# RWKV recurrence: values centred per head ahead of the scan, one mask instruction for both matrices of a bank, head norms and rates in two row halves

## The chip, the cores and the metric

The kernel runs on one core of a Trainium2 chip. The metric is the device time of one execution in microseconds (us); lower is better. Three runs of the kernel before took 3750.63, 3755.2 and 3758.21 us, a median of 3755.2 us.

## The reference

The reference is a two-block network over 512 positions of width 1024 with 256 context positions. One block mixes by attention, the other by an RWKV-7 recurrence with 16 heads of 64 values, in both directions; each has a feed-forward part. What the change touches is this part of the second block:

```python
def wkv_scan(r, w, k, v, a, b, s0, reverse):
    def step(s, inp):
        r_t, w_t, k_t, v_t, a_t, b_t = inp
        sa = jnp.einsum('bhvk,bhk->bhv', s, a_t)
        s = s * w_t[:, :, None, :] + sa[..., None] * b_t[:, :, None, :] + v_t[..., None] * k_t[:, :, None, :]
        return s, jnp.einsum('bhvk,bhk->bhv', s, r_t)
...
    a = heads(jax.nn.sigmoid((a0 + (xa @ a1) @ a2).astype(F32)))
    kk = k * k_k.astype(F32).reshape(hn)
    kk = kk / jnp.maximum(jnp.sqrt(jnp.sum(kk * kk, axis=-1, keepdims=True)), 1e-12)
...
def group_norm(y, g, b):
    mean = jnp.mean(y, axis=-1, keepdims=True)
    var = jnp.mean(jnp.square(y - mean), axis=-1, keepdims=True)
    return (y - mean) * lax.rsqrt(var + GN_EPS) * g.astype(F32).reshape(hn) + b.astype(F32).reshape(hn)
```

The output of the scan is normalized per head over its 64 values. The scan is linear in `v`, and its state starts at zero, so that the mean over a head's values of `y` is the scan's answer to the mean of `v`. Values with their mean taken off give an output whose mean is zero.

## The kernel before

The second block's mixer runs in stages, each of which works on eight pairs of heads (128 of the 1024 channels, 768 positions of context and sequence).

- **k projection**, then **features**. `rwkv_features` runs the v and r projections (`psk`, three matmuls for each product of numbers split in a high and a low half) on TensorE, and weaves into them the features of one head pair after another: `psrn` (head norms, spread from the rows of `rnT` by a 32-row matmul), `psa` (rates, from `ta`, a 64-row matmul), `psw` (decays; its two 64-row halves alternate in pieces of 256 columns), `psgt`, `psbon`. The results go to scratch tensors in DRAM (`scr_bk`, `scr_ax`, `scr_ac`, `scr_v`, `scr_z`).
- **Transition**. `rwkv_wkv` takes new SBUF for the recurrence, loads the first pair (`BK`, `DA`, `DC`, `v`) on POOL's and SP's queues, and runs its scores. On POOL's queue behind these stand 16 loads of 512 KB of the weights `ada_w`, which a small product (`psada`) uses.
- **Recurrence**. For pair p, `in_order` deals out the steps of several generators by the table `WKV_ORDER` (`WKV_LAST` for the last pair): matmuls `m`, cross terms `y`, transfer `w` (which makes `FC` and `FT`), the scan `s` of pair p, the readout `z` of pair p-1 (group norm, then the gate), scores `g` and fills `a`, `b`, `v` of later pairs. Between them it spreads the 34 steps of `wkv_inverse` for pair p+1, which runs on VectorE (DVE): it copies 32x32 blocks of the triangular matrices `GA` into `Z`, transposes them into `T` (L2067, L2068), adds 1 to the diagonal (L2070), inverts them by 30 steps of a product `pr` and a sum into `T` (L2077, L2078), transposes back into `TC` and `TS`, and copies out to `TTt`.
- `wkv_scores` makes 20 masked matrices a pair out of 12 PSUM banks `psg`: 12 of `GA` (L1988) and 8 of `E` (L1990), each 128x256.
- `wkv_fill_v` turns the values around by TensorE transposes into `UV` (L2008). `wkv_readout` takes mean (L2235, L2236), difference (L2238, on POOL), square (on ACT), variance (L2242), scales `Y` (L2247), transposes it (`psz`), makes `z` (L2258), multiplies it into `zz` (L2260, on POOL) and adds both directions (L2262). For the last pair these go to DVE.
- **Readout and what follows** use the recurrence's output through `scr_o`.

Of the kernel before, what the change touches and what calls it, by code (L numbers as in the profile page):

```python
# [9 lines left out]
F32 = mybir.dt.float32  # L10
# [8 lines left out]
P = 128  # L19
# [1422 lines left out]
def host_consts3():  # L1442
    f = np.float32
    c = {}
    p = np.arange(P)
    same = (p[:, None] // 64) == (p[None, :] // 64)
    q, k = (p % 64)[:, None], np.arange(64)[None, :]
    m = np.zeros((P, 2, 2, 64), f)
    m[:, 0, 0], m[:, 0, 1] = q <= k, q < k
    m[:, 1, 0], m[:, 1, 1] = q >= k, q > k  # L1450
    c["k_rmask"] = m
    c["k_bones"] = same.astype(f)

    head = np.zeros((P, KT, 32), f)
    headT = np.zeros((3, 32, 3, P), f)
    for a in range(KT):
        for h in range(2):
            head[64 * h:64 * h + 64, a, 2 * (a // 3) + h] = 1
            headT[:, 2 * (a // 3) + h, a // 3, 64 * h:64 * h + 64] = 1
    c["k_head"], c["k_headT"] = head, headT.reshape(96, 3, P)  # L1460
    return c
# [7 lines left out]
WKV_LAST = "y m y m y y z w w z m w m z s w w s z w s z s w w w s s z s z z s z s r s q s q s q s q s"  # L1469
# [23 lines left out]
class Net3(Net2):  # L1493
# [13 lines left out]
    def rwkv_proj(self, x, scr):  # L1507
# [5 lines left out]
        nc.sync.dma_start(self.mask, A["k_rmask"])  # L1513
        M = XW - 2
# [4 lines left out]
        with ExitStack() as s, ExitStack() as s0:  # L1519
            lo_ = self.pool(s, "lora", 1)  # L1520
            tw = self.tw = lo_.tile([P, TT], F32, name="tw")
            ta = self.ta = lo_.tile([64, TT], F32, name="ta")
            rnT = lo_.tile([96, TT], F32, name="rnT")
# [13 lines left out]
            with ExitStack() as s1, ExitStack() as s2:  # L1537
# [18 lines left out]
                for gi, ps_ in enumerate(([0, 1, 2], [3, 4, 5], [6, 7])):  # L1556
# [30 lines left out]
                    for (_, dc, wd), z in zip(segs, ss):  # L1587
                        for j, (p, sq) in enumerate(zip(ps_, sqs)):
                            nc.tensor.matmul(z[32 * j:32 * j + 32, :], lhsT=hd[:, p, :], rhs=sq[:, dc:dc + wd], start=gi == 0, stop=gi == (1 if j == 2 else 2))
                for (_, dc, w), z in zip(segs, ss):  # L1590
                    nc.scalar.sqrt(rnT[:, dc:dc + w], z[0:96, :])
# [70 lines left out]
    def feature_setup(self, s):  # L1662
# [8 lines left out]
        f["headT"] = headT = sp.tile([96, 3, P], F32, name="headT")  # L1671
# [33 lines left out]
    def features(self, p, r, rnT):  # L1705
# [3 lines left out]
        hr = slice(32 * (p % 3), 32 * (p % 3) + 32)  # L1709
# [94 lines left out]
    def rwkv_wkv(self, rest):  # L1804
        nc, A = self.nc, self.A
        with ExitStack() as s:
# [5 lines left out]
            self.E = [cp.tile([P, 5, 2, 8, 64], F32, name=f"E{d}") for d in range(2)]  # L1812
# [219 lines left out]
    def wkv_fill_m(self, u):  # L2032
        nc, GA, UV = self.nc, u["GA"], u["UV"]
        for (s0, n) in ((8, 4), (0, 8)):
            for h in range(2):
                ps = self.psum("psmv")
                for i in range(n):
                    sl = s0 + i
                    for d in range(2):
                        q, kh = slice(64 * d, 64 * d + 64), slice(64 - 64 * d, 128 - 64 * d)  # L2040
                        nc.tensor.matmul(ps[q, i * 64:(i + 1) * 64], lhsT=GA[d][kh, h, sl, :], rhs=UV[kh, h, sl, d, :], start=True, stop=True)
# [16 lines left out]
    def wkv_inverse(self, u):  # L2058
        nc, tl, Z, GA, TTt = self.nc, self.wt, self.Z, u["GA"], self.TTt
# [25 lines left out]
        for d in range(2):  # L2085
            for bl in range(2):
# [3 lines left out]
                put(TTt[q, :, :, 64 * d + 32 * bl:64 * d + 32 * bl + 32], src[q, :, 0:24].rearrange("p t (h s) -> p h s t", h=2))  # L2090
# [131 lines left out]
    def wkv_readout(self, u, parts=((0, 8),)):  # L2222
        nc, tl, psum = self.nc, self.rt, self.psum
        Y, pc = u["Y"], u["pc"]
        side = nc.vector if u["p"] == KT - 1 else nc.gpsimd
        mn, vr = (tl([P, 16], n, 2) for n in ("mn", "vr"))
# [3 lines left out]
        for j0, j1 in parts:  # L2230
            e = slice(2 * j0, 2 * j1)
            y3 = Y[:, j0:j1].rearrange("p j d t -> p (j d) t")
            m, v, q = mn[:, e], vr[:, e], sq[:, e]
# [15 lines left out]
            for d in range(2):  # L2249
# [10 lines left out]
                side.tensor_tensor(zz[:, d, cs], zz[:, d, cs], z, MUL)  # L2260
# [113 lines left out]
```

## Time and profile before

| | before |
|---|---|
| runs (us) | 3750.63, 3755.2, 3758.21; median 3755.2 |
| profiled execution (us) | 3759.0, span 3757.2 |
| PE busy | 3554.0 us (95%) |
| DVE busy | 2065.8 us (55%) |
| ACT busy | 1531.4 us (41%) |
| POOL busy | 726.0 us (19%) |
| the chain that ended last | PE 53%, DVE 9%, ACT 2%, issue 2%, DMA 1% of the span |

The table is read by stage: features last from 1205 to 1365 us of the span, the transition to 1420, the recurrence from there to 1860. Busy shares over the whole span say little on a stage of them.

### The profile page before, as it was taken

The numbers are of one execution on the slowest core, as the hardware profiler recorded it, in microseconds if no ns is written. First come the engines' busy times: TensorE is split into PE (matmuls) and PEld (weight loads), VectorE is DVE, ScalarE is ACT, GpSimd is POOL, SyncE is SP. The second block draws the span as 40 slices with busy tenths as digits, with TensorE's granted clock in tenths as the row PEclk, the third lists the DMA queues.
The fourth block names the chain that finished last, engine by engine and source line by source line (L and its number), as shares of the span: only waits on it lengthen the run. The fifth ranks groups of instructions, "written<-read, shape, count | busy, mean of one in ns | idle before, by whom it ended". The sixth has DMA issues, their size and how long they took to land.

```text
span 3757.2 us, 63564 instructions
## 1 busy us (share of the span) xinstructions
PE 3554.0 (95%) x26108; PEld 2920.4 (78%) x26108; DVE 2065.8 (55%) x3937; ACT 1531.4 (41%) x2956; POOL 726.0 (19%) x588
## 2 busy tenths in 40 slices
PE   7999999999989988889799999998999899989998
PEld 5767877888865657777588889988888799978886
DVE  5556433333457778899454345567444744573346
ACT  5556332222234655556442234354222345442233
POOL 2100033433222010001224440003111200031112
PEclk9999999999989998888899999999999999989999
DMA  5132233222222782322433332122333321223332
GB/s 182 61 103 95 68 99 104 64 65 62 73 88 71 277 298 91 92 80 87 157 118 95 96 95 91 57 63 87 103 97 90 96 64 60 78 79 100 97 95 68
DMA packets 308211, 370.80 MB, mean 99 GB/s; under 512 B 31712, under 2 KB 228304, under 8 KB 305872
## 3 DMA queue, kind: packets, MB, share of 16 engines
q1 hardware_dynamic: 298752, 340.28, 28.7%
q0 software_dynamic: 8912, 26.39, 2.2%
q8 instruction: 205, 3.36, 0.4%
q14 instruction: 86, 0.70, 0.1%
q10 hardware_dynamic: 256, 0.07, 0.0%
HBM read 324.71 MB, written 41.98 MB: 98 GB/s over the span
## 4 chain that ended last, share of the span: by engine, by line
PE 53%; DVE 9%; ACT 2%; issue 2%; DMA 1%; POOL 0%; SPq 0%; DVEq 0%; ACTq 0%; POOLq 0%
PE psu L142 5%; PE psu L141 5%; PE psu L140 5%; PE psy L142 5%; PE psy L140 4%; PE psy L141 4%; PE psj L140 4%; PE psj L142 4%; PE psj L141 4%; DVE T L2078 1%; DVE Tlo L296 1%; DVE pr L2077 1%; PE S L972 1%; PE psk L140 1%; PE psk L141 1%
## 5 line engine op out<-in xcount | busy, mean ns | idle before, releaser
L135 DVE TENSOR_TENSOR wlo<-wraw,whi 128x1024 fp32r<-128x1024 f32 (+1 forms) x402 | 505.3, 1259 | 543.1 <-ACT whi L134 542.4
L134 ACT CAST whi<-wraw 128x1024 fp32r<-128x1024 f32 (+1 forms) x402 | 417.1, 1039 | 920.2 <-PE psy L142 528.2
L140 PE MATMUL psu<-Thi,whi 128*128 128x512 f32 (+1 forms) x1408 | 499.9, 355 | 8.7 <-ACT r L332 6.0
L142 PE MATMUL psu<-Thi,wlo 128*128 128x512 f32 (+1 forms) x1408 | 501.1, 356 | 0.3 <-DVE wlo L135 0.3
L141 PE MATMUL psu<-Tlo,whi 128*128 128x512 f32 (+1 forms) x1408 | 499.6, 355 | 0.0
L140 PE MATMUL psj<-whi,Thi 128*128 128x256 f32 (+1 forms) x1568 | 482.9, 310 | 10.4 <-ACT whi L134 7.6
L142 PE MATMUL psj<-whi,Tlo 128*128 128x256 f32 (+1 forms) x1568 | 473.8, 303 | 2.5 <-DVE Tlo L296 2.5
L141 PE MATMUL psj<-wlo,Thi 128*128 128x256 f32 (+1 forms) x1568 | 474.3, 303 | 1.2 <-DVE wlo L135 1.0
L140 PE MATMUL psy<-whi,uh 128*128 128x512 f32 x1152 | 452.7, 393 | 3.3 <-ACT whi L134 2.0
L142 PE MATMUL psy<-whi,ul 128*128 128x512 f32 x1152 | 455.0, 395 | 0.0
L141 PE MATMUL psy<-wlo,uh 128*128 128x512 f32 x1152 | 452.3, 393 | 0.0
L333 POOL TENSOR_TENSOR q<-r 128x512 f32<-128x512 f32 (+1 forms) x176 | 235.3, 1337 | 880.0 <-ACT r L332 880.0
L140 PEld LDWEIGHTS psj<-whi,Thi 128*128 128x128 f32 x1568 | 300.2, 192 | 27.4 <-ACT whi L134 9.5
L142 PEld LDWEIGHTS psj<-whi,Tlo 128*128 128x128 f32 x1568 | 299.6, 191 | 15.0 <-DVE Tlo L296 4.2
L141 PEld LDWEIGHTS psj<-wlo,Thi 128*128 128x128 f32 x1568 | 300.3, 192 | 13.0 <-DVE wlo L135 2.5
L140 PEld LDWEIGHTS psu<-Thi,whi 128*128 128x128 f32 x1408 | 268.3, 191 | 52.1 <-ACT r L332 8.1
L141 PEld LDWEIGHTS psu<-Tlo,whi 128*128 128x128 f32 x1408 | 268.4, 191 | 40.7
L142 PEld LDWEIGHTS psu<-Thi,wlo 128*128 128x128 f32 x1408 | 268.3, 191 | 38.5 <-DVE wlo L135 0.7
L335 DVE TENSOR_TENSOR ul<-q,uh 128x512 fp32r<-128x512 f32 (+1 forms) x176 | 105.0, 597 | 316.4 <-ACT uh L334 316.1
L142 PEld LDWEIGHTS psy<-whi,ul 128*128 128x128 f32 x1152 | 216.8, 188 | 53.2 <-DVE ul L335 6.5
L140 PEld LDWEIGHTS psy<-whi,uh 128*128 128x128 f32 x1152 | 216.7, 188 | 52.3 <-ACT whi L134 2.4
L141 PEld LDWEIGHTS psy<-wlo,uh 128*128 128x128 f32 x1152 | 216.9, 188 | 47.2
(545 smaller groups left out, 6100.8 us busy)
## 6 DMA issues: line engine op xcount, KB each, us to landing
wraw<-in_mlp_w_dram SPq DMA_DIRECT2D x128, 512.0 KB, 3.9
wraw<-in_ffn_w_dram SPq DMA_DIRECT2D x128, 512.0 KB, 3.8
wraw<-in_ada_w_dram SPq DMA_DIRECT2D x64, 512.0 KB, 4.8
wraw<-in_ev_w_in_dram SPq DMA_DIRECT2D x28, 512.0 KB, 3.6
scr_bk<-BK SPq DMA_DIRECT2D x16, 768.0 KB, 3.3
wraw<-in_od_w_in_dram SPq DMA_DIRECT2D x24, 512.0 KB, 3.6
BK<-scr_bk SPq DMA_DIRECT2D x14, 768.0 KB, 4.7
wraw<-in_rwkv_w_rkv_dram SPq DMA_DIRECT2D x16, 512.0 KB, 4.6
```

The lines of the kernel that those rows point to most:

```text
L134: nc.scalar.copy(hi, raw)
L135: nc.vector.tensor_tensor(lo, raw, hi.bitcast(F32), SUB)
L140: mm(ps, lhsT=ah, rhs=bh, start=start, stop=False)
L141: mm(ps, lhsT=ah, rhs=bl, start=False, stop=False)
L142: mm(ps, lhsT=al, rhs=bh, start=False, stop=stop)
L296: nc.vector.tensor_tensor(lo[k][:, s], t[:, :w], hi[k][:, s].bitcast(F32), SUB)
L333: nc.gpsimd.tensor_tensor(q[:, :w], r[:, :w], r[:, :w], MUL)
L335: nc.vector.tensor_tensor(ul[:, o:o + w], q[:, :w], uh[:, o:o + w].bitcast(F32), SUB)
L972: nc.tensor.matmul(S[e][:, c], lhsT=q[r], rhs=k[r, c], start=True, stop=True)
L2077: nc.vector.tensor_tensor(pv, T[:, j + 1:, j:j + 1].to_broadcast([P, n, j]), T[:, j:j + 1, 0:j].to_broadcast([P, n, j]), MUL)
L2078: nc.vector.tensor_tensor(T[:, j + 1:, 0:j], T[:, j + 1:, 0:j], pv, ADD)
```

## The change

1. Features: `psa` and `psrn` are made together. `rnT` moves into rows 64 to 127 of a tile whose rows 0 to 63 hold `ta`, the table `headT` goes to 64 rows, and the two 64-row matmuls alternate in pieces of 256 columns. The sums of squares that fill `rnT` (`ss`) take columns 64 and 96 in place of 0, 32 and 64.
2. Values: `wkv_fill_v` multiplies by `cent` (the unit matrix less 1/64 within each head) in place of a transpose. The readout loses mean, its scaling, and the difference.
3. Masks: `GA` of the 8 sequence chunks moves into two more slots of `E`, so that one instruction of 512 elements masks both matrices of a bank. `GAc` holds the 4 context chunks. Each copy into `Z` and out to `TTt` becomes two, for 8 and 4 chunks.
4. Inverse: the first and the last of the 30 steps become one instruction each, and the diagonal is set to 1 by a memset after the first.
5. The product into `zz` goes from POOL to DVE for all pairs. `WKV_LAST` has one `q` less.
6. SBUF: each `E` grows from 5 to 7 slots (4 KB each per partition), `GA` gives way to the smaller `GAc`. By that the tiles that are allocated behind `E` start later.

```diff
-            self.E = [cp.tile([P, 5, 2, 8, 64], F32, name=f"E{d}") for d in range(2)]
+            self.E = [cp.tile([P, 7, 2, 8, 64], F32, name=f"E{d}") for d in range(2)]
...
         for (o, w) in segs:
-            ps = psum("psrn")
-            nc.tensor.matmul(ps[:, :w], lhsT=f["headT"][hr, p // 3, :], rhs=rnT[hr, o:o + w], start=True, stop=True)
-            nc.vector.scalar_tensor_tensor(na[:, o:o + w], in0=k[:, o:o + w], scalar=f["nkk"][:, pc], in1=ps[:, :w], op0=MUL, op1=MUL)
-        yield
-        for (o, w) in segs:
-            ps = psum("psa")
-            nc.tensor.matmul(ps[:, :w], lhsT=a2, rhs=self.ta[:, o:o + w], start=True, stop=True)
-            nc.scalar.activation(ic[:, o:o + w], ps[:, :w], AF.Tanh, bias=f["ha0"][:, pc], scale=0.5)
-        nc.scalar.activation(ic, ic, AF.Copy, bias=0.5, scale=0.5)
-        yield
+            pa, pn = psum("psa"), psum("psrn")
+            for c in range(0, w, 256):
+                for ps, l, rhs in ((pa, a2, self.ta), (pn, f["headT"][:, p, :], rnT)):
+                    nc.tensor.matmul(ps[:, c:c + 256], lhsT=l, rhs=rhs[:, o + c:o + c + 256], start=True, stop=True)
+            nc.scalar.activation(ic[:, o:o + w], pa[:, :w], AF.Tanh, bias=f["ha0"][:, pc], scale=0.5)
+            nc.vector.scalar_tensor_tensor(na[:, o:o + w], in0=k[:, o:o + w], scalar=f["nkk"][:, pc], in1=pn[:, :w], op0=MUL, op1=MUL)
...
-                    nc.vector.tensor_tensor(GA[d][:, h, sg4, :], pv[:, :, n - 1, :], mask[:, d, 1, :].unsqueeze(1).to_broadcast([P, 4, 64]), MUL)
-                    if n == 2:
-                        nc.vector.tensor_tensor(self.E[d][:, u["R"][d], h, sg4, :], pv[:, :, 0, :],
-                                                mask[:, d, 0, :].unsqueeze(1).to_broadcast([P, 4, 64]), MUL)
+                    if n == 1:
+                        nc.vector.tensor_tensor(GAc[d][:, h], pv[:, :, 0, :], mask[:, d, 1, :].unsqueeze(1).to_broadcast([P, 4, 64]), MUL)
+                    else:
+                        a, b = u["R"][d], u["A"]
+                        nc.vector.tensor_tensor(self.E[d][:, a:b + 1:b - a, h, sg4, :], pv.rearrange("p s e t -> p e s t"),
+                                                mask[:, d].unsqueeze(2).to_broadcast([P, 2, 4, 64]), MUL)
...
-                nc.tensor.transpose(ps[:, i * P:(i + 1) * P], v[:, c * 64:c * 64 + 128], self.ident)
+                nc.tensor.matmul(ps[:, i * P:(i + 1) * P], lhsT=v[:, c * 64:c * 64 + 128], rhs=self.cent, start=True, stop=True)
...
-                put(Z[q, :, 0:24], GA[d][q, :, :, 32 * bl:32 * bl + 32].rearrange("p h s t -> p t (h s)"))
+                put(Z[q, :, 0:16], self.E[d][q, u["A"], :, :, cs].rearrange("p h s t -> p t (h s)"))
+                put(Z[q, :, 16:24], u["GAc"][d][q, :, :, cs].rearrange("p h s t -> p t (h s)"))
...
-        dg = T.rearrange("p a b -> p (a b)")[:, 0:1024:33]
-        nc.vector.tensor_scalar(dg, dg, 1.0, None, ADD)
...
+            if j in (1, 30):
+                out = T[:, 2:, 0] if j == 1 else T[:, 31, 0:30]
+                nc.vector.scalar_tensor_tensor(out, in0=T[:, 2:, 1] if j == 1 else T[:, 30, 0:30], scalar=T[:, 1, 0:1] if j == 1 else T[:, 31, 30:31],
+                                               in1=out, op0=MUL, op1=ADD)
...
-            nc.vector.tensor_reduce(m, y3, AX.X, ADD)
-            nc.vector.tensor_scalar(m, m, 1.0 / 64, None, MUL)
-            yield
-            side.tensor_tensor(y3, y3, all64(m), SUB)
-            yield
...
-                side.tensor_tensor(zz[:, d, cs], zz[:, d, cs], z, MUL)
+                nc.vector.tensor_tensor(zz[:, d, cs], zz[:, d, cs], z, MUL)
```

Three places show how the instructions move. The first is TensorE in the features of one head pair, first before (`psk` are projection matmuls, the numbers behind names are of buffers):

```order
L1723 MATMUL psrn<-rnT,headT 128x512
L1723 MATMUL psrn<-rnT,headT 128x256
L140 MATMUL psk<-vh,whi 128x512
L141 MATMUL psk<-vl,whi 128x512
L142 MATMUL psk<-vh,wlo 128x512
L1728 MATMUL psa<-ta,a_11578 128x512
L1728 MATMUL psa<-ta,a_11578 128x256
```

The same two products of another head pair with the change:

```order
L1732 MATMUL psa<-tarn,a_10842 128x256
L1732 MATMUL psrn<-tarn,headT 128x256
L1732 MATMUL psa<-tarn,a_10842 128x256
L1732 MATMUL psrn<-tarn,headT 128x256
...
L1732 MATMUL psa<-tarn,a_10842 128x256
L1732 MATMUL psrn<-tarn,headT 128x256
```

Two matmuls of each, on 32 and on 64 rows, have become three of each on 64 rows, which alternate.

The second is VectorE in the recurrence, from the transposes that end one inverse to those that begin the next, before (the part around the second head's masks is left out):

```order
L2083 STREAM_TRANSPOSE TS<-T 128x1024
L1988 TENSOR_TENSOR GA_15602<-psg,rmask 128x256
L1990 TENSOR_TENSOR E_12152<-psg,rmask 128x256
...
L2064 COPY Z<-GA_15602 32x32x24 x2
L2067 STREAM_TRANSPOSE T<-Z 64x1024
...
L2235 TENSOR_REDUCE mn<-Y 128x16
L2068 STREAM_TRANSPOSE T<-Z 64x32x32
L2236 TENSOR_SCALAR mn<-mn 128x16
L2107 COPY y1s<-psy_15917 32x384
L2070 TENSOR_SCALAR T<-T 128x32
```

The same place with the change:

```order
L2106 STREAM_TRANSPOSE TS<-T 128x1024
L2003 TENSOR_TENSOR E_12169<-psg,rmask 128x2x256 x2
...
L2079 COPY Z<-E_12169 32x32x16 x2
L2083 STREAM_TRANSPOSE T<-Z 64x1024
L2000 TENSOR_TENSOR GAc_15586<-psg,rmask 128x256 x2
L2003 TENSOR_TENSOR E_12170<-psg,rmask 128x2x256 x4
L2084 STREAM_TRANSPOSE T<-Z 64x32x32
L2091 SCALAR_TENSOR_TENSOR T<-T 128x30
L2132 COPY y1s<-psy_15895 32x384
L2095 MEMSET T 128x32
```

The mean and the sum on the diagonal are gone, and the `Z` copies of the context chunks (not in these rows) stand between steps of the inverse before.

The third is VectorE where `z` of a pair meets the inverse, with the change; before, `L2258 z` stood here without the product behind it:

```order
L2178 TENSOR_TENSOR FT<-psft,IR 128x512 x2
L2101 TENSOR_TENSOR T<-T,pr 128x14x17
L2277 SCALAR_TENSOR_TENSOR z<-psz,ncol,bv 128x512
L2100 TENSOR_TENSOR pr<-T 128x234
L2279 TENSOR_TENSOR zz<-zz,z 128x512
L2101 TENSOR_TENSOR T<-T,pr 128x13x18
L2281 TENSOR_TENSOR zz<-zz 128x512
```

The product `zz<-zz,z`, an instruction of POOL before, now stands among the steps on VectorE.

## Rows read from the trace of the kernel before

**Rows 1.** Windows by stage: us, busy of PE, PEld, DVE, ACT, POOL, clock, DMA share, GB/s.

```profile
1250.00:1300.00 50.00, 50.00 (x232) 34.86 (x231) 39.01 (x51) 34.77 (x54) 0.00 (x0) 1.00 0.79 264
...
1350.00:1400.00 50.00, 39.60 (x342) 26.64 (x342) 37.14 (x80) 25.48 (x40) 12.43 (x20) 0.86 0.99 365
...
1519.84:1576.83 56.99, 50.24 (x962) 43.78 (x958) 49.60 (x109) 31.68 (x72) 4.52 (x3) 0.82 0.29 88
...
1632.33:1687.00 54.67, 46.95 (x966) 40.99 (x966) 49.59 (x106) 31.49 (x73) 4.51 (x3) 0.91 0.29 92
```

**Rows 2.** Chain that ended last, features: start, us on the chain, what.

```profile
1260.38 1.48 PE psrn L1723 x4
...
1262.76 1.48 PE psa L1728 x4
...
1268.09 1.06 PE psw L1738 x8
...
1270.04 0.63 PE psw L1738 x4
```

**Rows 3.** Timeline of POOL and PE, transition: start, us, operation, [idle before, releaser].

```profile
1348.67 0.53 POOL L1939 DMA_DIRECT2D DA<-scr_ax  x1
...
1364.03 2.09 POOL L221 DMA_DIRECT2D E<-in_ada_w_dram  x4 [14.30 <-DMA scr_z<-gt]
...
1365.93 0.71 PE L1979 MATMUL psg<-DA,BK 64*128 64x128 f32 x4 [1.34 <-ACT vf L1639]
...
1373.16 2.40 PE L1979 MATMUL psg<-DA,BK 64*128 64x128 f32 x16 [4.28 <-DVE GA L1988]
```

**Rows 4.** DMA issues from 1340 to 1370: queue, count, KB, us to landing.

```profile
DA<-scr_ax POOLq DMA_DIRECT2D x1, 1024.0 KB, 14.8
```

**Rows 5.** Timeline of DVE in one period of the recurrence, 1632 to 1687.

```profile
1633.81 0.41 DVE L1990 TENSOR_TENSOR E<-psg,rmask 128x256 f32<-128x256 f32 x1
1634.14 0.41 DVE L1988 TENSOR_TENSOR GA<-psg,rmask 128x256 f32<-128x256 f32 x1
...
1648.04 1.22 DVE L2235 TENSOR_REDUCE mn<-Y 128x16 f32<-128x1024 f32 x1 [1.85 <-ACT Y L2218]
1649.59 1.93 DVE L2068 STREAM_TRANSPOSE T<-Z 64x1024 f32<-64x1024 f32 x1 [0.33 <-ACT Z L2064]
...
1652.34 1.48 DVE L2070 TENSOR_SCALAR T<-T 128x32 f32<-128x32 f32 x1
...
1670.13 1.28 DVE L2153 TENSOR_TENSOR FT<-psft,IR 128x512 f32<-128x512 f32 x2
...
1672.41 1.36 DVE L2078 TENSOR_TENSOR T<-T,pr 128x240 f32<-128x240 f32 x1
1673.81 0.41 DVE L2077 TENSOR_TENSOR pr<-T 128x238 f32<-128x238 f32 x1
...
1682.11 0.68 DVE L2262 TENSOR_TENSOR zz<-zz 128x512 f32<-128x512 f32 x1
```

**Rows 6.** Timeline of POOL and ACT in the same period.

```profile
1651.87 1.90 POOL L2238 TENSOR_TENSOR Y<-Y,mn 128x1024 f32<-128x1024 f32 x1 [25.02 <-ACT y1s L2106]
1672.20 1.31 POOL L2260 TENSOR_TENSOR zz<-zz,z 128x512 f32<-128x512 f32 x1 [18.43 <-DVE z L2258]
...
1648.04 1.52 ACT L2064 COPY Z<-GA 32x768 f32<-32x768 f32 x1
```

**Rows 7.** Timeline of PE in the recurrence, two periods.

```profile
1518.97 0.66 PE L2008 MATMUL psv<-ident,v 128*128 128x128 f32 x4
...
1526.35 1.11 PE L2008 MATMUL psv<-ident,v 128*128 128x128 f32 x4
...
1670.71 2.05 PE L2132 MATMUL pswu<-RH,TTt 128*128 128x128 f32 x16
```

**Rows 8.** Chain that ended last, last pair and tail.

```profile
1826.14 1.88 POOL Y L2238
...
1851.76 1.28 POOL zz L2260
```

More of the change, by code (lines that the diff above doesn't have):

```diff
@@ L1452, in host_consts3 @@
     c["k_bones"] = same.astype(f)
+    c["k_cent"] = (np.eye(P) - same / 64.0).astype(f)
     head = np.zeros((P, KT, 32), f)
-    headT = np.zeros((3, 32, 3, P), f)
+    headT = np.zeros((64, KT, P), f)
     for a in range(KT):
         for h in range(2):
-            head[64 * h:64 * h + 64, a, 2 * (a // 3) + h] = 1
-            headT[:, 2 * (a // 3) + h, a // 3, 64 * h:64 * h + 64] = 1
-    c["k_head"], c["k_headT"] = head, headT.reshape(96, 3, P)
+            head[64 * h:64 * h + 64, a, 2 * (a // 2) + h] = 1
+            headT[32 * (a % 2) + 2 * (a // 2) + h, a, 64 * h:64 * h + 64] = 1
+    c["k_head"], c["k_headT"] = head, headT
     return c
@@ L1513, in rwkv_proj @@
         nc.sync.dma_start(self.mask, A["k_rmask"])
+        self.cent = self.keep.tile([P, P], F32, name="cent")
+        nc.sync.dma_start(self.cent, A["k_cent"])
         M = XW - 2
@@ L1521, in rwkv_proj @@
             tw = self.tw = lo_.tile([P, TT], F32, name="tw")
-            ta = self.ta = lo_.tile([64, TT], F32, name="ta")
-            rnT = lo_.tile([96, TT], F32, name="rnT")
+            both = lo_.tile([P, TT], F32, name="tarn")
+            ta, rnT = both[:64], both[64:]
+            self.ta = ta
             sg = self.sg = lo_.tile([P, 2, SX], F32, name="sg")
@@ L1587, in rwkv_proj @@
                     for (_, dc, wd), z in zip(segs, ss):
-                        for j, (p, sq) in enumerate(zip(ps_, sqs)):
-                            nc.tensor.matmul(z[32 * j:32 * j + 32, :], lhsT=hd[:, p, :], rhs=sq[:, dc:dc + wd], start=gi == 0, stop=gi == (1 if j == 2 else 2))
+                        for p, sq in zip(ps_, sqs):
+                            j = 64 + 32 * (p % 2)
+                            nc.tensor.matmul(z[j:j + 32, :], lhsT=hd[:, p, :], rhs=sq[:, dc:dc + wd], start=p < 2, stop=p >= KT - 2)
                 for (_, dc, w), z in zip(segs, ss):
-                    nc.scalar.sqrt(rnT[:, dc:dc + w], z[0:96, :])
+                    nc.scalar.sqrt(rnT[:, dc:dc + w], z[64:, :])
                 nc.vector.tensor_scalar(rnT, rnT, 1e-12, None, MAX)
@@ L1967, in wkv_scores @@
         BK, DA, DC, mask = u["BK"], u["DA"], u["DC"], self.mask
-        u["GA"] = GA = [self.gp.tile([P, 2, NSLOT, 64], F32, name=f"GA{d}", tag=f"GA{d}") for d in range(2)]
+        u["GAc"] = GAc = [self.gp.tile([P, 2, 4, 64], F32, name=f"GAc{d}", tag=f"GAc{d}") for d in range(2)]
         for d in range(2):
@@ L2040, in wkv_fill_m @@
                         q, kh = slice(64 * d, 64 * d + 64), slice(64 - 64 * d, 128 - 64 * d)
-                        nc.tensor.matmul(ps[q, i * 64:(i + 1) * 64], lhsT=GA[d][kh, h, sl, :], rhs=UV[kh, h, sl, d, :], start=True, stop=True)
+                        nc.tensor.matmul(ps[q, i * 64:(i + 1) * 64], lhsT=self.aref(u, d, kh, h, sl), rhs=UV[kh, h, sl, d, :], start=True, stop=True)
                 nc.scalar.copy(u["RH"][:, h, s0:s0 + n, 64:128], ps[:, :n * 64].rearrange("p (s t) -> p s t", t=64))
@@ L2058, in wkv_inverse @@
     def wkv_inverse(self, u):
-        nc, tl, Z, GA, TTt = self.nc, self.wt, self.Z, u["GA"], self.TTt
+        nc, tl, Z, TTt = self.nc, self.wt, self.Z, self.TTt
         for d in range(2):
@@ L2074, in wkv_inverse @@
             n = 31 - j
-            pr = tl([P, 256], "pr")
+            if j in (1, 30):
+                out = T[:, 2:, 0] if j == 1 else T[:, 31, 0:30]
+                nc.vector.scalar_tensor_tensor(out, in0=T[:, 2:, 1] if j == 1 else T[:, 30, 0:30], scalar=T[:, 1, 0:1] if j == 1 else T[:, 31, 30:31],
+                                               in1=out, op0=MUL, op1=ADD)
+                if j == 1:
+                    nc.vector.memset(T.rearrange("p a b -> p (a b)")[:, 0:1024:33], 1.0)
+                yield
+                continue
+            pr = tl([P, 240], "pr")
             pv = pr[:, :n * j].rearrange("p (a b) -> p a b", b=j)
@@ L2100, in wkv_cross @@
             for sl in range(NSLOT):
-                i = h * NSLOT + sl
+                i = h * 8 + sl if sl < 8 else 16 + h * 4 + sl - 8
                 c = slice(32 * sl, 32 * sl + 32)
-                nc.tensor.matmul(y1[q1, c], lhsT=GA[0][q0, h, sl, 32:64], rhs=TS[q0, :, i], start=True, stop=True)
-                nc.tensor.matmul(y1[q2, c], lhsT=GA[1][q3, h, sl, 0:32], rhs=TC[q3, :, i], start=True, stop=True)
+                nc.tensor.matmul(y1[q1, c], lhsT=self.aref(u, 0, q0, h, sl)[:, 32:64], rhs=TS[q0, :, i], start=True, stop=True)
+                nc.tensor.matmul(y1[q2, c], lhsT=self.aref(u, 1, q3, h, sl)[:, 0:32], rhs=TC[q3, :, i], start=True, stop=True)
             y1s = tl([P, SX], "y1s", 2)[:, :NSLOT * 32]
@@ L2224, in wkv_readout @@
         Y, pc = u["Y"], u["pc"]
-        side = nc.vector if u["p"] == KT - 1 else nc.gpsimd
-        mn, vr = (tl([P, 16], n, 2) for n in ("mn", "vr"))
+        vr = tl([P, 16], "vr", 2)
         sq = tl([P, 16, 64], "ysq", tag="ro")
```

23 lines of the change are left out of this document (15 added, 8 removed).

## The prediction

> **What bounds the kernel now.** I read the windows by stage first, because the share of the whole span averages over stages with different limits. In the features, 1250 to 1300, TensorE (PE) is busy 50.00 of 50 us at the full clock, VectorE (DVE) 39.01, ACT 34.77 and the DMA engines 0.79 of the time: the stage ends when PE has gone through its list [rows 1]. The chain of that stage is PE throughout, and it holds for each head pair 1.48 us of psrn, 1.48 of psa, and 1.06 and 0.63 of psw [rows 2]. In the transition, 1350 to 1400, PE has 39.60 busy and DVE 37.14, but DMA is at 0.99 and moves 365 GB/s: that stage is as long as its bytes [rows 1]. In the recurrence, a period of 54.67 us holds 49.59 us of DVE and 46.95 of PE, ACT 31.49; another holds 49.60 of DVE and 50.24 of PE in 56.99 us, at a clock of 0.82 in place of 0.91 [rows 1]. So DVE, with its inverse, leads there by little, and PE stands close behind it. Six periods have this form, from 1465 to about 1800.
>
> **The change part by part.** The sum is made against the profiled execution's own 3759.0 us, which is 3.8 above the median of the runs, 3755.2.
>
> *Features.* psw moves twice the columns of psa (two 64-row halves that alternate) and takes 1.06 + 0.63 = 1.69 us, little more than psa alone [rows 2]. The new pair of psa and psrn has just that form and column count, so 1.48 + 1.48 becomes 1.69: 1.27 us less for each head pair. PE has no idle time there, so this counts in full. There are 8 pairs; I count 7, since the first stands where the weave with the projection only begins: 8.9 us. The bound below is none at all (the halves do not overlap and psw is quick for another reason), above it 8 pairs, 10.2. DVE at 39 of 50 would be at 39 of 47, ACT lower; neither takes over. The matmuls of `ss` are the same number, at other columns, and come out even.
>
> *Transition.* Before, the first load of DA went out at 1348.67, well before the projections were over, and was 14.8 us on the way [rows 3, 4]. The larger E pushes DA, DC and v into SBUF that still holds the high half of v's input (`vh`), read by the last projection matmuls. So DA now waits for the end of PE's list; before, PE went idle 1.34 us ahead of the first psg at 1365.93, that is at 1364.6 [rows 3]. With the shift of 8.9 the issue falls to about 1355.7. Behind it on POOL's queue stand DC and then the loads of ada_w, the first of which went out at 1364.03 after a wait for the last of the features' stores [rows 3]. DA's 1024 KB thus move out of a stretch with DMA time to spare (0.79 in the window before) into one that is full; at 365 GB/s they take 2.9 us. I take 8.9 - 2.9 = 6.0 gained over features and transition. The lower end: DA lands 14.8 after 1355.7, at 1370.5, which is 4.6 later than psg began before. PE waited 4.28 us for DVE's masks shortly after [rows 3], so that such a delay is just covered, and the gain there is 0. The upper end is 8.9. What DVE saves in the first pair's inverse does not count, since DMA ends that stage; for the rest of the first pair I take 1 (0 to 2).
>
> *Recurrence, one period.* On DVE:
> - T beside POOL: while POOL's product zz ran from 1672.20 for 1.31, a T step of 240 elements took 1.36; the step of 238 next to it took 0.41 [rows 5, 6]. POOL has two of these a period, and the second lands on a T step too: 2 x 0.95 = -1.9.
> - The sum on the diagonal took 1.48, beside POOL's difference of 1.90 which began 0.47 ahead of it [rows 5, 6]. A memset of its 32 elements takes its place; I give it 0.3, under the 0.41 of a step of 238: -1.2.
> - The mean, 1.22 (L2235), stands in a wait: DVE was idle 1.85 ahead of it and 0.33 behind it, until ACT had both Z copies of 768 elements, 1.52 each [rows 5, 6]. With the context part copied earlier, 512 elements each are left, 1.0 each by size: the wait ends 1.0 earlier. So the mean itself gives nothing, and this -1.0. Its scaling, 16 elements, at half of that 0.41: -0.2.
> - Masks: two of 256 elements take 0.74 (0.33 to the next start, then 0.41), one of 512 from PSUM takes 0.64 by FT's two in 1.28 [rows 5]. Eight pairs of them by 0.1, less the stride that the two operands now have: -0.5.
> - First and last step of the inverse, an instruction less each, of 30 elements, at the same 0.2: -0.4.
> - The product zz comes to DVE, two of 512 elements by 0.68 as the sum of zz shows [rows 5], less the overlap: +1.2. Half copies of Z and TTt, four more instructions: +0.3.
>
> Together -3.7. On PE: four psv transposes take 0.66, and eight full matmuls on the same 128x128 f32 shape (pswu, 16 instructions, two for each) 2.05 [rows 7]. That is 0.15 against 0.26, +0.1 each, 12 a period: +1.2. At the lower clock four transposes took 1.11 [rows 7]; if the matmul grows alike, +2.4. Part of it lies in PE's 7.7 idle us of a period, part on the chain, as PE hands the chain to DVE and back: I take 0.7. That leaves -3.0 a period. Bounds: -3.7 + 2.4 = -1.3, all of it on the path; and -4.5, where PE hides it and the earlier ysq also ends a wait. Six periods: -18 (-8 to -27).
>
> Here a rule speaks against the change. The Trainium skill, Perfetto Trace Analysis, section Optimizing Tensor Performance (Transposes), wants a logical transpose done as a transpose and not as a standard matmul; TensorE: Matmul & The Clock Gate, section Terms, calls transpose mode 4 times as fast for FP32. By it a psv matmul would cost 0.59 and the period 5.3 us more of PE; the rows above show 1.7 times, not 4.
>
> *Last pair and tail.* POOL's difference stood on the chain with 1.88 and its product with 1.28 [rows 8]. The first goes; the second becomes 0.68 on DVE: -2.5. The readout has two steps less to wait its turn for: -0.5. I take -3 (-1 to -5).
>
> Sum: -6.0 - 1 - 18 - 3 = -28, that is 3731.0 on the profiled time and 3727 against the median.
>
> **The rivals.**
> - *The late DA eats the features' gain* (DMA 0.99 speaks for it, PE's 4.28 us of cover against it): -22, 3733.
> - *PE takes over in the recurrence.* For it: PE's 50.24 beside DVE's 49.60 in one period, and TC and TS now follow each other, 3.2 us in which DVE frees no score bank. Then -1.3 a period: -6 - 1 - 8 - 3 = -18, 3737. With the rival above, 3743.
> - *psv costs four transposes.* By the price of four of them, 0.66, for each matmul, PE gets 12 x 0.5 = 6 us more a period and passes 53 to 56: the recurrence gains nothing, -6 - 3 = -9, 3746. pswu's rate speaks against it.
> - *Slower: the clock.* A period at clock 0.82 lasted 56.99, one at 0.91 54.67 [rows 1]. If PE waits longer behind TC and TS and is granted the lower clock in all six, the period grows by 2.3 instead of falling: +14, less the tail's 3 and the features' 6 or 0: +5 to +11, 3760 to 3766. It decides once the added wait a period is more than the 3.0 saved. [...]
> - *All of it counts*: -8.9 - 2 - 27 - 5 = -43, 3712.
> - *The halves do not overlap*: no gain in features, and DA still late: -21, 3734.
>
> **How the numbers follow.** Forecast 0.42; late DA 0.14; PE takes over 0.14, both 0.06; psv by four 0.04; no overlap 0.05; all counts 0.11; slower 0.04. 0.2% of this kernel, 7.5 us, is about what a measurement can tell from no change. Same comes from the edges of the cases at 3743 and 3746 and a part of the clock's: 0.07; slower 0.04; faster 0.89. The range takes in the bounds of all terms, 3712 less 2 and 3747.
>
> **What would show it.** The pair psa and psrn at about 1.7 us and 1.3 less between head pairs; DA issued only when the projections end, and the first psg waiting for DMA; no POOL work in the recurrence, no T step over 0.45; the wait for ACT's Z shorter by a microsecond; two TC 52 apart rather than 55; four psv at 1.0. The forecast is wrong if PE is then the longer of the two in a period, if the end of the transition doesn't come earlier by some 6, or if the clock of a period falls.

## The result and the profile after

The changed kernel took 3730.61 us (median of 4 runs, 3728.78 to 3737.26) against 3754.34 before (a fourth run of it took 3753.47): a ratio of 0.994, with a 95% interval of 0.9924 to 0.9956. That is 24 us less, where 28 were forecast. The profiled execution is the slowest of the four, 3737.26, so stages are compared below within a profile, from landmark to landmark, and totals by the medians.

Windows of the changed kernel by stage, with the columns of [rows 1]; the last two are periods of the recurrence, from one TC to the next (TC and TS are the transposes that end an inverse):

```profile
1250.00:1300.00 50.00, 50.00 (x249) 36.26 (x247) 42.20 (x57) 36.02 (x54) 0.00 (x0) 1.00 0.85 290
...
1350.00:1400.00 50.00, 34.20 (x331) 25.01 (x330) 37.50 (x77) 21.08 (x36) 13.61 (x22) 0.80 0.87 317
...
1567.74:1619.71 51.97, 46.78 (x982) 40.87 (x982) 45.63 (x103) 32.50 (x76) 0.00 (x0) 0.97 0.30 96
1619.71:1674.04 54.33, 50.81 (x982) 44.65 (x982) 45.80 (x103) 33.00 (x76) 0.00 (x0) 0.87 0.30 93
```

The features are still TensorE's alone. The window from 1350 to 1400 has lost its full DMA (0.87 for 0.99), which is the first sign that something there waits that did not. In the recurrence DVE fell from 49.6 to 45.7, POOL is empty, and the two periods shown differ: 52.0 us at a granted clock of 0.97, and 54.3 at 0.87, where PE is busy 4 us more on the same instructions.

The features' timeline on PE, one head pair, and the psbon that ends two successive pairs:

```profile
1341.25 0.48 PE L1732 MATMUL psa<-tarn,a 64*128 64x256 f32 x1
1341.26 0.48 PE L1732 MATMUL psrn<-tarn,headT 64*128 64x256 f32 x1
1341.57 0.38 PE L1732 MATMUL psa<-tarn,a 64*128 64x256 f32 x1
...
1242.22 1.02 PE L1802 MATMUL psbon<-rk,bones 128*128 128x512 f32 x2
...
1262.84 1.02 PE L1802 MATMUL psbon<-rk,bones 128*128 128x512 f32 x2
```

psa and psrn start 0.01 apart: the halves run together. From pair to pair 20.62 us pass, where 21.90 had passed (psbon at 1243.76 and 1265.66).

The transition, where [rows 3] stood, on POOL and PE:

```profile
1340.70 1.09 POOL L1945 DMA_DIRECT2D BK<-scr_bk  x2 [138.08 <-PE psk L142]
1356.09 0.53 POOL L1946 DMA_DIRECT2D DA<-scr_ax  x1 [14.30 <-DVE sig L1763]
...
1397.42 1.06 POOL L221 DMA_DIRECT2D E<-in_ada_w_dram  x2 [13.14 <-PE psada L223]
...
1362.46 1.19 PE L1990 MATMUL psg<-DA,BK 64*128 64x128 f32 x4 [5.81 <-DMA DA<-scr_ax]
...
1391.12 1.13 PE L1993 MATMUL psg<-DC,BK 64*64 64x64 f32 x32 [8.40 <-DMA DC<-scr_ac]
```

DA goes out 15 us behind BK instead of right behind it; the row names a scan on DVE (`sig`) that ended just then, but the last projection matmuls end within 0.3 us of it, right ahead of psbon at 1355.63. The two keep this distance in every profile, so that time alone does not tell them apart; the place does: in the kernel's SBUF layout DA now starts on the first byte of `vh`, which those matmuls read, and `sig` lies elsewhere. PE then waits twice: 5.81 us for DA, and 8.40 for DC of the second pair. Behind the second wait stand the psada steps, and behind these POOL's next loads of ada_w. Windows of 10 us show what DMA does meanwhile:

```profile
1350.00:1360.00 10.00, 6.65 (x36) 4.20 (x34) 7.22 (x9) 7.37 (x13) 3.24 (x7) 0.97 0.73 278
...
1390.00:1400.00 10.00, 8.88 (x91) 5.50 (x92) 6.75 (x17) 1.17 (x2) 1.06 (x2) 0.65 0.61 218
```

In a stage that was as long as its bytes before (DMA at 0.99 [rows 1]), 0.27 and 0.39 of 10 us are lost, 6.6 us together.

On DVE and PE in a period, the rows that answer to [rows 5] and [rows 7]:

```profile
1622.68 1.25 DVE L2003 TENSOR_TENSOR E<-psg,rmask 128x512 f32<-128x512 f32 x2
...
1637.02 1.95 DVE L2084 STREAM_TRANSPOSE T<-Z 64x1024 f32<-64x1024 f32 x1 [2.22 <-ACT Z L2079]
1639.00 0.28 DVE L2091 SCALAR_TENSOR_TENSOR T<-T 128x30 f32<-128x30 f32 x1
...
1639.96 0.09 DVE L2095 MEMSET T<- 128x32 f32 x1
```

```profile
1619.48 1.16 PE L2022 MATMUL psv<-cent,v 128*128 128x128 f32 x8
1620.57 0.45 PE L2215 MATMUL pstep<-S,FT 64*64 64x64 f32 x8
...
1623.38 0.66 PE L2041 MATMUL psat<-ident,DA 128*128 128x128 f32 x4 [1.72 <-DVE E L2003]
```

Four psv take 1.09 to the next instruction, for about 0.6. Who waits for whom has shifted. These are DVE's waits for scores over the six periods before, and its two largest waits after (engine, instruction, releaser: us in total, times, longest):

```profile
DVE GA L1988 <- PE psg L1979: 3.4, 3, 2.2
DVE GA L1988 <- PE psg L1982: 0.9, 2, 0.6
```

```profile
DVE E L2003 <- PE psg L1990: 17.1, 12, 2.5
DVE T L2084 <- ACT Z L2079: 13.3, 6, 2.2
```

Before, DVE waited 4.3 us in all for scores. Now it waits 17.1: DVE spends part of what it saved on waiting for PE.

### The profile page after: what moved, and what is told of

Same layout as the page of the kernel before. It is cut to its first block, busy times and chain, and to the rows that moved or that the text cites. A ratio compares the mean times of both kernels' runs of the same rounds, so it can differ in the third digit from the quotient of the medians.

```text
span 3735.5 us, 63689 instructions
## 1 busy us (share of the span) xinstructions
PE 3543.6 (95%) x26236; PEld 2921.2 (78%) x26236; DVE 2035.9 (55%) x3883; ACT 1537.1 (41%) x2988; POOL 694.5 (19%) x567
## 4 chain that ended last, share of the span: by engine, by line
PE 81%; DVE 10%; DMA 4%; ACT 3%; issue 2%; POOL 0%; SPq 0%; ACTq 0%; DVEq 0%; POOLq 0%
PE psy L142 7%; PE psy L140 7%; PE psu L142 7%; PE psy L141 7%; PE psu L140 7%; PE psu L141 7%; PE psj L140 5%; PE psj L142 5%; PE psj L141 5%; PE po L579 2%; PE psk L140 1%; PE S L535 1%; DVE Tlo L296 1%; PE pst L554 1%; PE psk L142 1%
## 5 line engine op out<-in xcount | busy, mean ns | idle before, releaser
L142 PEld LDWEIGHTS psj<-whi,Tlo 128*128 128x128 f32 x1568 | 299.7, 191 | 14.8 <-DVE Tlo L296 4.2
```

The costliest lines, as they stand in the source:

```text
L142: mm(ps, lhsT=al, rhs=bh, start=False, stop=stop)
```

## The experiments

All ran against the kernel before, whose medians beside them were 3754.56, 3754.64 and 3752.53; each has its ratio to it. An interval is some 3 to 6 us to either side, so small differences are read from the profiles' stages. The table gives spans of each profile between landmarks on PE and DVE, in us: from the first psk to the last psbon (k projection and features), from there to psadat (the small product's last step: transition), from there to the last TC (recurrence), and from there to the first psu of the feed-forward part (last pair and tail).

| kernel | median | ratio, interval | to psbon | to psadat | to last TC | to psu |
|---|---|---|---|---|---|---|
| before | 3754.34 | 1 | 310.9 | 57.4 | 375.9 | 122.4 |
| changed | 3730.61 | 0.994, 0.9924 to 0.9956 | 304.5 | 64.6 | 361.5 | 118.7 |
| f_only | 3748.42 | 0.9982, 0.9973 to 0.9992 | 304.4 | 58.7 | 376.2 | 122.0 |
| r_only | 3739.84 | 0.9963, 0.995 to 0.9976 | 311.8 | 63.2 | 361.2 | 119.5 |
| b_da | 3730.01 | 0.9932, 0.9918 to 0.9947 | 304.5 | 59.5 | 358.7 | 122.8 |
| b_da_ord | 3727.18 | 0.9927, 0.9916 to 0.9939 | 304.9 | 54.2 | 359.9 | 119.8 |
| x_mean | 3735.92 | 0.9956, 0.9944 to 0.9968 | 304.5 | 63.6 | 359.8 | 120.0 |
| x_ident | 3717.90 | 0.9903, 0.9888 to 0.9918 | 304.8 | 63.5 | 346.1 | 117.5 |
| x_double | 3734.55 | 0.9953, 0.9941 to 0.9966 | 304.4 | 63.2 | 359.5 | 117.9 |
| x_zzpool | 3744.54 | 0.9971, 0.9962 to 0.998 | 304.5 | 63.9 | 368.7 | 121.7 |
| x_ts | 3734.80 | 0.9951, 0.9938 to 0.9963 | 304.9 | 66.8 | 359.3 | 115.8 |
| x_mask | 3733.09 | 0.9951, 0.9937 to 0.9965 | 304.9 | 65.5 | 359.0 | 117.2 |
| best3 | 3729.98 | 0.9943, 0.9931 to 0.9956 | 305.0 | 54.3 | 359.6 | 122.4 |
| best3d | 3720.78 | 0.9919, 0.9905 to 0.9932 | 304.4 | 54.6 | 354.8 | 124.2 |

Kernels with the same instructions in a stage show how far one profile can be trusted. The transition of the changed kernel and of the seven others with its placing lasts 63.2 to 66.8. The recurrence of changed, r_only, b_da and b_da_ord, which is the same, lasts 358.7 to 361.5, and their last stretch 118.7 to 122.8; the two together vary less, 479.8 to 481.5, against 498.4 before and 498.2 in f_only.

**Where the features' gain went.** f_only is the kernel before with the features' part alone. r_only is the changed kernel with psrn and psa apart again:

```diff
-            pa, pn = psum("psa"), psum("psrn")
-            for c in range(0, w, 256):
...
+            pn = psum("psrn")
+            nc.tensor.matmul(pn[:, :w], lhsT=f["headT"][:, p, :], rhs=rnT[:, o:o + w], start=True, stop=True)
...
+        for (o, w) in segs:
+            pa = psum("psa")
+            nc.tensor.matmul(pa[:, :w], lhsT=a2, rhs=self.ta[:, o:o + w], start=True, stop=True)
```

Expected of f_only: 

> Theory A: the features gain 6 to 8 us on TensorE (1.27 a pair), and the changed kernel gives them back in the transition because DA, DC and v wait for the last projection matmul. Here only the features are changed and DA lies where it lay before: the first TC should come 6 to 7 us earlier than before, and the time should be 3748, 6 to 7 below before. Rival B: the transition is as long as its DMA bytes, whatever is ahead of it: the time is that of before within 1.5 us. Rival C: the halves do not overlap: psa with psrn takes 2.9 a pair and nothing is gained.

Expected of r_only: 

> The changed kernel with psrn and psa made one after the other again (each on its 64 rows, in pieces of 512 and 256 columns), all else as changed. Theory A: the features last as long as before and DA still waits for their end, so that the transition ends 6 to 8 us later than in the changed kernel: 3738. Rival B (bytes alone): the time of the changed kernel within 1.5 us, 3731. psa and psrn at 1.48 each.

b_da puts DA, DC and v back over the r projection's input:

```diff
-            self.E = [cp.tile([P, 7, 2, 8, 64], F32, name=f"E{d}") for d in range(2)]
+            self.E = [cp.tile([P, 7, 2, 8, 64], F32, name="E0")]
+            self.GAc = [[cp.tile([P, 2, 4, 64], F32, name=f"GAc{d}{i}") for d in range(2)] for i in range(2)]
...
+            self.E.append(self.pool(s, "wc2", 1).tile([P, 7, 2, 8, 64], F32, name="E1"))
```

Expected of it: 

> The changed kernel with DA, DC and v moved back over the r projection's input (E1 and GAc change places with them). Theory A: the first psg no longer waits 5.8 us for DA, the wait for DC later shrinks, the first TC comes 3 to 7 us earlier than in the changed kernel: 3724 to 3728. Rival B: no change, 3731 within 1.5. A further possibility: the second wait (psg for DC of the next pair, 8.4 us) stays, then only 3 of the 7 come back.

b_da_ord also moves steps `c` (psada) ahead of `g` (scores of the second pair):

```diff
-WKV_START = "l A A A v v v k c c . . . g g a g g c a g g c a g g c g g c g g c c c c"
+WKV_START = "l A A A v v v k c c . . . c c g g a g g a c g g a c g g c g g g g c c c"
```

Expected of it: 

> As b_da, and in the order of the transition the next two steps of psada stand ahead of the scores of the second pair, so that the loads of ada_w behind them are issued while TensorE would wait for DC. Theory A: DMA idles less between 1390 and 1400, and the first TC comes another 2 to 4 us earlier than in b_da. Rival B: the same time as b_da within 1.5.

With the features alone the gain arrives: psadat comes 5.2 us earlier (310.9 + 57.4 against 304.4 + 58.7) and the median falls by 6. Bytes did not bind it, so rival B fell. In r_only the pair apart costs 7.3 us up to psbon and the transition is still long, 63.2. With DA, DC and v back in their places (E1 and `GAc` give way to them, the instructions are the same), the transition is 5.1 us shorter than the changed kernel's 64.6, and 3.7 below the shortest of the eight with DA late. POOL and PE of b_da show why:

```profile
1342.51 1.09 POOL L1947 DMA_DIRECT2D BK<-scr_bk  x2 [138.14 <-PE psk L142]
1343.60 0.53 POOL L1948 DMA_DIRECT2D DA<-scr_ax  x1
...
1359.58 0.71 PE L1992 MATMUL psg<-DA,BK 64*128 64x128 f32 x4 [1.34 <-ACT vf L1646]
...
1387.96 1.14 PE L1995 MATMUL psg<-DC,BK 64*64 64x64 f32 x32 [4.46 <-DMA DC<-scr_ac]
```

DA goes out with BK again, psg waits 1.34 as before the change, the wait for DC halves, and DMA is full from 1350 to 1360, where the changed kernel has 0.73. Where the time goes shows when each step is counted from the last psbon, in us:

| | before | changed | b_da |
|---|---|---|---|
| first psg | 2.4 | 6.8 | 2.4 |
| first psada | 24.4 | 25.2 | 24.4 |
| load of the second pair's DC goes out | 20.8 | 25.2 | 21.1 |
| psg on that DC | 29.4 | 35.5 | 30.7 |
| psadat | 57.4 | 64.6 | 59.5 |

The changed kernel starts its scores 4.5 late and has made up all but 0.8 of that by psada; the loss comes at the second pair's DC. The new order takes the transition down by another 5.3, to 54.2, shorter than before the change. In total the two are at the edge of what the runs separate: b_da's median is only 0.6 below the changed kernel's, its five runs lying between 3723 and 3734, so that by the total alone rival B is not excluded.

**What the centring costs.** x_ident takes transposes in `wkv_fill_v` again, x_double takes each of them twice. Both leave the centring out, so that their output lacks the subtraction of the mean: they price PE's instructions only.

```diff
-                nc.tensor.matmul(ps[:, i * P:(i + 1) * P], lhsT=v[:, c * 64:c * 64 + 128], rhs=self.cent, start=True, stop=True)
+                nc.tensor.transpose(ps[:, i * P:(i + 1) * P], v[:, c * 64:c * 64 + 128], self.ident)
```

Expected of x_ident: 

> The changed kernel with the values turned by transposes again, and not centred (the output lacks the mean's subtraction). Prices psv: four in 0.6 in place of 1.09, 1.5 us of PE less a period. Theory: PE's added 1.5 lies half on the path, 0.5 to 1 a period less: 3724 to 3728. Rival: PE has room and DVE bounds: 3730 within 1.5. Rival: the transposes lower the granted clock and it gets slower: over 3734.

Expected of x_double: 

> As the run with transposes in place of centring matmuls (3717.9), but every transpose done twice into the same place, so that four chunks take about 1.2 us of PE again, as the four matmuls did (1.09), by transposes alone (the values are not centred). Theory: PE's time as such is what the centring cost, as PE bounds stretches of the recurrence: 3728 to 3732, periods of 52 to 54.4. Rival: matmuls cost otherwise than by their time (the granted clock falls where they stand): stays at 3716 to 3721, periods at 51.1.

x_ident is 12.7 us faster by the medians, about twice the most that was expected of it; in the profiles the span is 18.4 shorter, 15.4 of it in the recurrence (346.1 for 361.5). x_double gives it back, and 2 to 3 us more than expected. So PE's time as such is the price, not the kind of instruction. A period of each, with the columns of [rows 1], first x_ident:

```profile
1613.59:1664.69 51.10, 46.64 (x972) 40.07 (x973) 45.70 (x102) 32.19 (x76) 0.00 (x0) 0.93 0.31 98
```

and x_double, where both periods of the changed kernel are back:

```profile
1568.19:1620.06 51.87, 46.58 (x983) 40.38 (x982) 45.63 (x102) 32.50 (x76) 0.00 (x0) 0.97 0.31 97
1620.06:1674.29 54.23, 50.60 (x983) 44.31 (x982) 45.81 (x103) 32.98 (x76) 0.00 (x0) 0.87 0.31 93
```

DVE is busy the same 45.7 in all three; what differs is PE's list and the clock that it is granted, 0.93, 0.97 and 0.87. The extra 1.5 us a period (12 times the difference of a quarter of 1.09 and of 0.59, at the full clock) cost 0.8 in the short form (51.1 to 51.9) and 3.1 in the long one; over seven pairs x_ident's 15.4 are 2.2 each.

**The mean.** x_mean puts mean, scaling and difference back:

```diff
+            nc.vector.tensor_reduce(v, y3, AX.X, ADD)
+            nc.vector.tensor_scalar(v, v, 1.0 / 64, None, MUL)
+            yield
+            side.tensor_tensor(y3, y3, all64(v), SUB)
+            yield
```

Expected: 

> The changed kernel with mean, scaling and difference put back into the readout (the values stay centred, so that they take off a mean of zero; WKV_LAST as before). My sum gave the mean itself nothing (it lay in a wait), its scaling 0.2, and the difference 1.2 through the diagonal's instruction beside it on POOL; in the last pair 1.9 on the chain. By that: 1 to 2 a period and 2 to 4 in the last pair, 3739 to 3747. Rival: DVE is the bound and all of the 1.4 counts besides, 3 a period: 3752. Rival: all hidden, 3731 to 3734.

It came out below its 3739 to 3747: 5.3 us above the changed kernel by the medians, but the intervals overlap. Its profile has DVE at 47.9 to 49.3 in the first five periods, 2 to 3 more, and is no longer from psadat to psu (479.8 for 480.2). There the mean is hidden, as in my sum: the short period is 52.0 in both. Whether the 5.3 are real is open.

**The product zz.** x_zzpool puts it back on POOL (`side.tensor_tensor` for `nc.vector.tensor_tensor`).

Expected: 

> The changed kernel with the product into zz back on POOL (all but the last pair). Theory (contention): two T steps a period take 0.95 more each and two products of 0.6 leave DVE, +0.7 a period: 3733 to 3736, with T steps of 1.3 to 1.4 in the profile. Rival: the products cost DVE more than the contention, -1 a period: 3724.

It is 13.9 us slower than the changed kernel, with intervals apart, where 2 to 5 were expected: the largest effect of any part. DVE's row beside POOL's second product (1.36 us from 1612.26):

```profile
1612.10 0.39 DVE L2101 TENSOR_TENSOR T<-T,pr 128x234 f32<-128x234 f32 x1
1612.52 1.35 DVE L2100 TENSOR_TENSOR pr<-T 128x228 f32<-128x228 f32 x1
1613.80 0.68 DVE L2282 TENSOR_TENSOR zz<-zz 128x512 f32<-128x512 f32 x1
1614.40 0.38 DVE L2101 TENSOR_TENSOR T<-T,pr 128x228 f32<-128x228 f32 x1
```

The step took 0.95 more, as in [rows 5]. Over the six periods x_zzpool has twelve steps of the inverse of 1.34 to 1.42, two a period, where the changed kernel has none over 0.45. The contention has its price, and the two products that leave DVE by it (1.2) do not make up for that. DVE's busy time rose by 1.1 a period, to 46.9. That is some 7 of the 13.9; PE's waits for FT from DVE rose besides from 3.4 to 16.9 us over the six periods, and how the rest comes about was not isolated.

**The masks.** x_mask makes two instructions of 256 out of each of 512.

Expected: 

> The changed kernel with each mask of 512 elements as two of 256 again, at the same place. The sum gave 0.5 a period for this: 8 x (0.74 - 0.64). By that 3734 (3732 to 3737), DVE busy 45.6 to 45.8 in a period up by 0.7 to 1.3. Rival: PE bounds, 3731 within 1.5.

DVE's busy time rose to between 46.2 and 46.4 in a period, by 0.4 to 0.6, as the sum had it (0.5) and less than the 0.7 expected of this run. The total moved by 2.5 us, inside the intervals, and the recurrence is no longer than the changed kernel's: the masks' share of the gain is not shown by it.

**The order of TC and TS.** x_ts lets TS wait for two masks (`issue_after` on the mask).

Expected: 

> The changed kernel with the transpose TS issued after the two masks of the bank that is ready then, as it stood before the change. Periods of the changed kernel are 52.0 at clock 0.97 or 54.3 at 0.87; my theory is that PE's wait of 1.7 us behind TC and TS (no mask frees a bank for 3.1 us) leads to the low clock some 15 us later. Then the wait shrinks to under 0.6 and most periods last 52 or less: 3720 to 3725. Rival: the clock falls for another reason, periods as in the changed kernel: 3729 to 3733.

Inconclusive: the masks did move between TC and TS, but PE is idle as long at that place, 3.02 at once and for ACT, where the changed kernel had 1.72 and 1.23; the periods stay 52.0 and 54.3:

```profile
1575.14 0.54 PE L2218 MATMUL pstep<-S,FT 64*64 64x64 f32 x8 [3.02 <-ACT S L2233]
```

So the idle time that I had blamed for the low clock was never taken away, and the theory was not tested.

**A version from the parts.** best3 joins b_da_ord with transposes and, on POOL as before, the mean's difference in the readout; best3d does the difference on DVE (`side = nc.vector`).

Expected of best3: 

> The version that the runs point to: DA moved back and the psada steps ahead of the second pair's scores, values by transposes and the mean in the readout again, the rest as changed (masks, inverse, zz on DVE, row halves). Adding the runs' differences to 3730.6: -3.4 for the transition, -12.7 for transposes, +5.3 for the mean: 3720 (3715 to 3726). Rival: with transposes the mean's 1.4 on DVE counts in full since PE no longer covers it, 7 x 1.5 more than the 5.3 or so: 3726 to 3731.

Expected of best3d: 

> The same with the difference on DVE in place of POOL: 1.2 us a period more on DVE, and no instruction of DVE beside POOL's 1.9. If the contention costs more than 1.2: 3714 to 3719; if not: 3722 to 3728.

best3 came out at 3730, as its rival had it: the parts do not add. Without the centring's PE time DVE leads again (in the chain of three of its periods T and pr alone hold 30%), and what is put on DVE counts. best3d, where only the engine of that difference changes, is 9 us faster by the medians, with intervals that touch. In best3 one step of the inverse a period stands beside POOL's difference (1.90 us from 1583.49) and takes 1.26 to 1.50:

```profile
1583.96 1.49 DVE L2093 SCALAR_TENSOR_TENSOR T<-T 128x30 f32<-128x30 f32 x1
```

The same instruction takes 0.25 to 0.28 in the changed kernel, and best3d has no step over 0.45. So DVE is busy no longer in best3d (47.8 to 47.9 us in the second to fifth period for 48.1 to 48.4), although it now does the difference too, 1.22. What else makes up the 9 was not isolated. At 3720.78 best3d is 32 us below before, and 10 below the changed kernel, with intervals that just overlap (0.9905 to 0.9932 and 0.9924 to 0.9956). b_da_ord, which centres ahead of the scan and is otherwise nearly alike, lies between best3 and best3d (ratios 0.9927, 0.9943 and 0.9919), and its interval overlaps both: which way of centring is better is not shown. A period of best3d:

```profile
1666.70:1717.51 50.81, 45.12 (x972) 39.20 (x968) 47.77 (x105) 32.92 (x77) 0.00 (x0) 0.97 0.31 99
```

## Where the prediction held and where it did not, step by step

The time fell inside the range, but two of the three signs of being wrong that the prediction named came true. PE is the longer of the two in all six periods (46.8 to 50.9 us busy against DVE's 44.7 to 45.9), and psadat, the end of the transition, comes 0.7 us earlier and not 6 (1420.23 for 1420.93). The clock, the third, rose in four periods and fell in two (0.91 to 0.87, 0.88 to 0.87). The reading that DVE led before was thin, too: PE was already the longer in three of the six periods (53.2 against 49.8, 50.2 against 49.6, 50.2 against 49.9), and the window of 54.67 in [rows 1] ends 0.5 ahead of the next TC, so that its period is 55.1.

- **Features, -8.9 on the weave: right**, and the pair's price exact (1.28 a pair measured, 1.27 forecast). From the first psrn to the last psbon the stage is 9.5 shorter (156.7 to 147.1 us).
- **"The matmuls of `ss` ... come out even": wrong.** Before, two of them on different columns stood next to each other and ran partly together. Now three projection matmuls stand between them, and each runs alone; why the new columns part them the runs do not show. The first row is of before, the others of after:

```profile
1084.38 2.16 PE L1589 MATMUL ss<-ksq,hd 128*32 128x512 f32 x8
```

```profile
1082.72 1.48 PE L1596 MATMUL ss<-ksq,hd 128*32 128x512 f32 x4
1085.01 1.48 PE L1596 MATMUL ss<-ksq,hd 128*32 128x512 f32 x4
```

  Two for 2.16 became two for 2.96. From the first psk of the k projection to the first psk of the r projection 121.5 us pass for 119.4, and to the first psrn 157.4 for 154.2; every run with this layout has 121.5 to 121.6 and 157.2 to 157.9. What the last 1.1 of the 3.2 are I have not isolated. So features and k projection gained 6.4, not 8.9.
- **Transition, 2.9 given back: the term that was mis-sized.** It gave back 7.2 (57.4 to 64.6), more than the features had left. The rival of the late DA is what happened, though by another way than it said. DA took 6.2 us and not 14.8, and the cover of 4.28 held: the late start of the scores was made up to 0.8 by psada. Missing was the second half: DMA stands idle while DA is held back, the second pair's DC lands late, PE's in-order wait for it holds back psada, which holds back POOL's loads, and DMA idles again in a stage that is made of bytes. b_da shows the placing to be worth 5.1 in its profile; b_da_ord shows that the order around DC was worth another 5.3. Whether the kernel before would gain by that order too was not run.
- **DVE's ledger of a period, -3.7: right.** Of the -3.7, 1.0 is a wait and not work, and the mean's 1.2 is left out as hidden, so that its entries in busy time come to -3.9; measured are 4.0 (49.6 to 50.0 before, 45.6 to 45.9 after, in the first five periods). The wait behind Y and Z with the mean in it went from 3.4 (1.85 + 1.22 + 0.33 [rows 5]) to 2.2 us. x_mask and x_zzpool confirm single entries, 0.4 to 0.6 for 0.5 and 0.95 for each step beside POOL.
- **PE, +1.2 of which 0.7 counts: too small.** The matmuls cost 1.5 a period at the full clock, and by x_ident 2.2 counted. The rival "PE takes over" is therefore half true: in the long form of a period PE is busy 50.8 of 54.3 us, DVE waits 17.1 us for scores over the six, and the single periods fall by 0.5 to 5.4 rather than by 3.0. Over the six periods the sum gave -18, the profile shows -14.2 (from 336.85, TC at 1460.03 to 1796.88, to 322.69). The Trainium skill's Perfetto Trace Analysis, section Optimizing Tensor Performance (Transposes), asks for a transpose in place of a standard matmul wherever a transpose is meant. x_ident agrees as far as PE goes, by 12.7 us, but it leaves the centring out, which here was the point of the matmul. The Trainium skill's TensorE: Matmul & The Clock Gate, section Terms, gives transpose mode as 4 times faster for FP32; the rows here show 1.8 times (0.59 against 1.09).
- **First pair, -1:** 0.3 (TC to TC 37.54 for 37.84).
- **Last pair and tail, -3:** 3.7, from the last TC to the first psu matmul of the feed-forward part (122.4 to 118.7). The size is not settled by that: r_only, b_da and b_da_ord, with the same tail, have 119.5 to 122.8.

The parts of the profile that the change touches add up to -6.4 + 7.2 - 0.3 - 14.2 - 3.7 = -17.4. The other 4 of the profile's 21.7 us (3757.2 to 3735.5) fall in stages that the change leaves alone: 1.6 ahead of the k projection, 2.8 behind psu. The 24 of the medians rest on three more executions, 5.5 to 8.5 us faster than the profiled one; how many of their periods were short ones is not known. So the direction held, and so did the mechanism of the features' pair and of DVE's ledger. That the total came within 4 of the 28 is in part luck: in the profiles the stages of the change gave 17.4, and what is missing there lies in the transition and `ss` (0.8 lost where 6 were to be gained) and in the recurrence (14.2 for 18), where PE's time counted for more than the 0.7 a period of the sum.

## What to carry to other kernels

A larger tile moves everything allocated behind it: look up which dead or living data the next stage's first load now lies over, and then follow its queue to the end, since in a stage that is bound by bytes a late load costs as much idle DMA as all that waits behind it in order, on the queue and on TensorE (here 7.2 us for a load that itself took 6.2). When work goes from the leading engine to the one close behind, price it at both engines: here 1.5 us of TensorE a period counted as 2.2, and the fastest version with the whole output does without them, though by no more than the intervals allow. Where two engines slow each other, a few instructions matter: putting the product back on POOL cost 14 us, about half of it in DVE's busy time.

## What the runs showed that was not expected

The period of the recurrence comes in two lengths in one execution, on the same instructions: 51.97 us at a granted clock of 0.97 and 54.33 at 0.87, with PE busy 46.78 and 50.81. Both start after the same idle time of PE at TC and TS (1.7 and 1.2 us), and in both the clock is 0.66 from 5 to 10 us into the period; in the long one a second stretch follows some 20 us into it, with a granted clock of 0.50 from 1640 to 1645 (the lower of the two levels, 1.2 GHz) and 0.55 to 1650, with PE busy throughout. What decides between them stays open, and a length between them occurs too (53.4 at 0.94 in b_da). With 1.5 us of PE less in a period (x_ident) the long form was gone from the third period on: 51.0, 51.1, 51.1, at a clock of 0.93.
